# Dilated attention inside a float32 trunk: scores of two steps issued together, transposes by query tile, one shared set of four banks, and the dilation-16 groups one step ahead

## The chip, the cores and the metric

The kernel runs on one core of a Trainium2 chip. The metric is the device time of one execution in microseconds. Engines go by short names: TensorE (PE in the profile, PEld for its weight loads), VectorE (DVE), ScalarE (ACT), GpSimd (POOL) and SyncE (SP, which issues DMA transfers). An instruction that needs another engine's result waits for a semaphore. PSUM is the memory that TensorE writes; here it is divided into eight banks of 512 float32 columns.

## The reference, cut to what matters

The model is a trunk of two layers for one sequence of 1024 positions with 1024 channels, everything in float32. A layer is a token mixer and a squared-ReLU MLP, each modulated by a conditioning vector. The first mixer is a gated spatial MLP, the second is attention over three dilation patterns, which is where the change lies:

```python
B_HEADS, B_HEAD_DIM = 16, 64
B_PATTERNS = ((128, 1), (512, 4), (2048, 16))          # (window, dilation)
qkv = (h @ w_qkv).reshape(B, S, N_PAT, 3, B_HEADS, B_HEAD_DIM)
...
# dilated_branch, for one pattern: positions are split by their remainder modulo the dilation;
# a block of `span` = window // dilation queries sees its own and the previous block of keys
s = einsum('bnqrhe,bnkrhe->bnrhqk', qb, kb) * E ** -0.5
s = where(valid, s - slopes * dilation * diff, NEG)
m = max(s); p = exp(s - m); l = sum(p)
o = einsum('bnrhqk,bnkrhe->bnqrhe', p / l, vb)
lse = m + log(l)
...
wts = softmax(stack(lses))                             # over the three patterns
o = sum(wts * stack(outs)); return o.reshape(B, S, -1) @ w_out
```

## The kernel before

**Stages.** The program runs the gated MLP mixer, the first squared-ReLU MLP, attention and the second squared-ReLU MLP one after the other. Large products are made from float32 values split in a high and a low part (three matmuls for each product), and by a scheme of seven instead of eight half-size products. `attention` starts with the values of all heads (`values_stage`). Then everything else of attention is woven into one stream.

**The stream.** `project` (L1262) makes q and k for 24 groups: 8 pairs of heads, and for each the patterns of dilation 16, 4 and 1 in this order (`g` = 2, 1, 0). It is a generator. Each `next(stream)` issues three matmuls (`psqk`, L1351) and whatever ends with them: copies of a product's bank by ScalarE (`part`, L1329) or additions by VectorE (L1339), the building of a later weight operand (`left`: a cast on ScalarE, L103, and a subtraction on VectorE, L104). In this text such a step of three matmuls is a *unit*. A group has 28 units. Products that belong to one sum accumulate in one bank, so a product can wait until the copy of the bank's earlier state is done.

**The order table.** Attention itself is written into a table, `todo[step][pos]`, with 7 positions a step and 4 steps a group. `at(step, pos)` appends a function to a place. The main loop goes through the table: at each place it runs the functions there and then one unit of the stream. Group `n` has `base = 4 * n`. So the work of group `n` runs beside the projection of a later group. Once the stream is exhausted, chains of the output projection (`psd_wo`) take the place of its units. Instructions passed to `pe()` keep the order in which they are written, on their own engine; the softmax instructions (`soft`) and the copies out of banks are not held in this way.

**One step of attention.** For the near patterns (`attend`, dilation 4 and 1) a step `m` has two query tiles of 128 rows. `scores(m)` (L1616) makes scores of both heads, in two `sc` banks. For each tile and head, `soft` follows: one VectorE reduction (L1528) and one ScalarE exponential (L1530). `transposes(m, e)` (L1627, L1631) turn the probabilities of head `e` on TensorE into a `tr` bank, and a copy (L1639) brings them to SBUF; before the change the two places are one step after the scores, at positions 4 and 5, and the tile is filled by key tile, so that it also needs the next query tile's probabilities. `weighted(m)` (L1656) multiplies with the values, into the `pv` bank. For dilation 16 (`attend_far`) there are two larger steps of 64 by 64 matmuls (L1549, L1560, L1571).

**The merge.** When the three patterns of a pair are done, `merge` reads back the softmax statistics through device memory (`mst`), computes the factors (L1704 to L1716), writes them out and loads them again broadcast over rows (`bc`, two buffers), scales the three outputs (L1732; one on GpSimd, two on VectorE), adds them (L1737) and splits the sum (L103, L104). This runs beside the next pair's dilation-16 group and the first steps of its dilation-4 group; the last pair's merge runs beside the output projection. Small side jobs multiply rows of the output weight and of the residual by vectors (L1786) at fixed places.

Of the kernel before, what the change touches and what calls it, by code (L numbers as in the profile page):

```python
# [18 lines left out]
P = 128  # L19
S = 1024  # L20
D = 1024
NT = S // P
KD = D // P
HALF = 512
# [12 lines left out]
def trunk(ctx: ExitStack, tc: tile.TileContext, x, c, ada_w, ada_b, ln_g, ln_b, a_w_in, a_b_in,  # L37
# [1170 lines left out]
    def attention(before):  # L1208
# [16 lines left out]
        with ExitStack() as ph:  # L1225
# [244 lines left out]

            open_psum(ph, "B", sc=2, tr=2, mm=2, mb=1, pv=1)
            qp = pool(ph, "attn", 2)
# [59 lines left out]
            def attend_far(n, oT_of):  # L1532
# [22 lines left out]
                def transposes(h):  # L1555
                    pst = bank("tr", f"pT_{hp}_{g}_{h}")
                    for e in range(2):
                        for j in range(2):
                            o = (2 * e + j) * P
                            pe(T.transpose(pst[:, o : o + P], state["p", h][e][:, j * P : (j + 1) * P], ident[:]))  # L1560
                    t = state["pT", h] = qp.tile([P, HALF], F32, name=f"pTs_{hp}_{g}_{h}", tag="pT", bufs=6)
                    A.copy(t[:], pst[:])

                def weighted(h):
                    sums = [bank(kind, f"pv{s}_{hp}_{g}_{h}") for s, kind in enumerate(("pv", "tr"))]
                    for j in range(2):
# [14 lines left out]
                for h in range(2):  # L1581
                    at(base + 2 * h + 1, 0)(lambda h=h: scores(h))
                    at(base + 2 * h + 2, 2)(lambda h=h: transposes(h))
                    at(base + 2 * h + 3, 0)(lambda h=h: weighted(h))

                @at(base + STEPS, 1)
                def statistics():
                    for b in range(2):
                        nc.sync.dma_start(st_dram[hp, g].rearrange("s e (q b n) -> q (s e) b n", b=2, n=NT)[:, :, b, :],
                                          state["stat"][64 * b : 64 * b + 64].rearrange("p s e n -> p (s e) n"))  # L1590

            def attend(n, oT_of):
# [5 lines left out]
                probs, pT, state = {}, {}, {}  # L1598
                blocks = {m: [(t, (g == 0 and t < NT - 1) or (g == 1 and t % 2 == 0)) for t in (2 * m, 2 * m + 1)] for m in range(STEPS)}

# [3 lines left out]
                def scores(m):  # L1604
                    if m == 0:
                        state["stat"], state["bias"] = new_state(n)
                    scb = [bank("sc", f"sc_{2 * hp + e}_{g}_{m}") for e in range(2)]
                    stat, used, spans = state["stat"], 0, []
                    for t in (2 * m, 2 * m + 1):
                        w = 2 * P if has[t] else P  # L1610
                        sl = slice(used, used + w)
                        used += w
                        k0 = (t - 1) * P if has[t] else t * P
                        for e in range(2):
                            rows = slice(e * HEAD, (e + 1) * HEAD)
                            pe(T.matmul(scb[e][:, sl], my["q"][rows, t * P : (t + 1) * P], my["k"][rows, k0 : k0 + w],  # L1616
                                        start=True, stop=True))
                            spans.append((t, e, w, sl))
                    for t, e, w, sl in spans:
                        pr = probs[e, t] = qp.tile([P, 2 * P], F32, name=f"p_{2 * hp + e}_{g}_{t}", tag="p", bufs=8)  # L1620
                        col = (t % 2) * 4 + t // 2 if g == 1 else t
                        soft(pr[:, 0:w], scb[e][:, sl], state["bias"][e][:, width - w :], stat, e, col)

                def flip(pst, m, e, o):
                    for t, nxt in blocks[m]:
                        pr = probs[e, t]
                        pe(T.transpose(pst[:, o : o + P], pr[:, P : 2 * P] if has[t] else pr[:, 0:P], ident[:]))  # L1627
                        pT[e, t] = o
                        o += P
                        if nxt:  # L1630
                            pe(T.transpose(pst[:, o : o + P], probs[e, t + 1][:, 0:P], ident[:]))  # L1631
                            o += P
                    return o

                def transposes(m, e):
                    pst = bank("tr", f"pT_{2 * hp + e}_{g}_{m}")
                    end = flip(pst, m, e, 0)
                    t = qp.tile([P, HALF], F32, name=f"pTs_{2 * hp + e}_{g}_{m}", tag="pT", bufs=6)
# [3 lines left out]
                def weighted(m):  # L1642
# [3 lines left out]
                    pv = state["pv"]  # L1646
                    pieces = []
                    if m == 2 and blocks[1][1][1]:
                        pieces.append((3, 4 * P, pT[0, 3] + P, P))
                    for t, nxt in blocks[m]:  # L1650
                        pieces.append((t, t * P, pT[0, t], P * (1 + (nxt and t % 4 < 3))))
                    for n_, (t, q0, o, w) in enumerate(pieces):
                        for e in range(2):
                            rows = slice(e * HEAD, (e + 1) * HEAD)
                            o_ = o - pT[0, t] + pT[e, t]
                            pe(T.matmul(pv[rows, q0 % HALF : q0 % HALF + w], my["v"][:, t, rows], pT["tile", e, t // 2][:, o_ : o_ + w],  # L1656
                                        start=m % 2 == 0 and n_ == 0, stop=m % 2 == 1 and n_ == len(pieces) - 1, skip_group_check=True))
# [9 lines left out]

                for m in range(STEPS):
                    at(base + m, 0)(lambda m=m: scores(m))
                    at(base + m + 1, 4)(lambda m=m: transposes(m, 0))  # L1670
                    at(base + m + 1, 5)(lambda m=m: transposes(m, 1))
                    at(base + 3 + m // 2 * 2, 0)(lambda m=m: weighted(m))

                @at(base + STEPS - (n == len(order) - 1), 6 if n == len(order) - 1 else 1)
                def statistics():
                    d, stat = st_dram[hp, g], state["stat"]
                    if g == 0:
                        pst = bank("tr", f"pstat_{hp}")
                        pe(T.transpose(pst[0:32, 0:P], stat[:].rearrange("p s e n -> p (s e n)"), ident[:]))
# [7 lines left out]
            def merge(hp, oTs):  # L1687
# [120 lines left out]
            def scaled_row(i):  # L1808
# [4 lines left out]

                @at(base + 2, 5)
                def store():
# [157 lines left out]
```

## Time and profile before

| what | value |
|---|---|
| median of 3 runs | 2616.63 us (2616.61 to 2620.3) |
| profiled execution, its own time | 2611.85 us |
| its span | 2610.1 us, granted TensorE clock 0.997 |
| up to the first unit in a row of the stream | 1207.15 us |
| stream of projection and attention, 1207.15 to 1863 | 655.85 us, TensorE busy 654.94 |
| end of attention's stream and output projection, 1863 to 1953 | 90.0 us, TensorE busy 86.18 |
| after it, to the end | 657.1 us, TensorE busy 642.25 |

In the profile's rows for instructions the columns are start, duration, engine, line, operation, output and inputs, shapes, and how many equal instructions follow one another; in square brackets stands how long the engine was idle before and what ended that. `x8` scores are four matmuls in the code, since each leaves two records. A row of the waits view has the waiting engine, tile and line, what it waited for, the total in us, the count and the longest. A row of the windows view has a stretch, its length, and the busy time of each engine in it.

### The profile page before, as it was taken

The numbers are of one execution on the slowest core, as the hardware profiler recorded it, in microseconds if no ns is written. First come the engines' busy times: TensorE is split into PE (matmuls) and PEld (weight loads), VectorE is DVE, ScalarE is ACT, GpSimd is POOL, SyncE is SP. The second block draws the span as 40 slices with busy tenths as digits, with TensorE's granted clock in tenths as the row PEclk, the third lists the DMA queues.
The fourth block names the chain that finished last, engine by engine and source line by source line (L and its number), as shares of the span: only waits on it lengthen the run. The fifth ranks groups of instructions, "written<-read, shape, count | busy, mean of one in ns | idle before, by whom it ended". The sixth has DMA issues, their size and how long they took to land.

```text
span 2610.1 us, 36711 instructions
## 1 busy us (share of the span) xinstructions
PE 2561.9 (98%) x13226; PEld 2058.5 (79%) x13226; DVE 1902.3 (73%) x3506; ACT 1267.7 (49%) x2448; POOL 132.8 (5%) x201
## 2 busy tenths in 40 slices
PE   6999999999999999999999999999999999999998
PEld 5788878887788888888777777777777888878886
DVE  6767798877879678444677677776669856577987
ACT  3333385555444445333555556655417655544432
POOL 1001000000000001011010101110100000000000
PEclk9999999999999999999999999999999999999999
DMA  8553346666955744442354445454953754594562
GB/s 267 164 158 110 126 140 228 226 222 226 333 174 189 229 140 151 153 156 97 91 151 128 109 125 152 124 148 134 337 153 114 232 176 155 172 331 153 187 208 80
DMA packets 327291, 453.37 MB, mean 174 GB/s; under 512 B 51468, under 2 KB 177844, under 8 KB 327108
## 3 DMA queue, kind: packets, MB, share of 16 engines
q1 hardware_dynamic: 314244, 406.45, 48.9%
q0 software_dynamic: 12864, 44.57, 4.8%
q8 instruction: 103, 1.69, 0.3%
q14 instruction: 80, 0.66, 0.1%
HBM read 342.33 MB, written 108.61 MB: 173 GB/s over the span
## 4 chain that ended last, share of the span: by engine, by line
PE 85%; DVE 7%; DMA 4%; ACT 2%; issue 1%; SPq 0%; DVEq 0%; ACTq 0%
PE psd L1095 23%; PE psqk L1351 17%; PE psua L937 10%; PE psv L1424 9%; PE psuc L937 5%; PE psu L329 3%; DMA adaw<-in_ada_w_dram 3%; PE psd_wout L329 3%; PE psd_wo L329 3%; PE psub L937 2%; PE sc L1616 2%; PE pv L1656 2%; PE psv L522 1%; PE pT L1627 1%; DVE right L104 1%; DVE left L104 1%
## 5 line engine op out<-in xcount | busy, mean ns | idle before, releaser
L1351 PE MATMUL psqk<-right,left 128*128 128x512 f32 x2016 | 521.9, 404 | 0.9 <-ACT part L1329 0.9
L1351 PEld LDWEIGHTS psqk<-right,left 128*128 128x128 f32 x2016 | 362.0, 188 | 93.2 <-issue 15.3
L937 PE MATMUL psua<-right,left 128*128 128x512 f32 x1536 | 365.8, 391 | 3.2 <-ACT right L103 1.8
L1095 PE MATMUL psd<-rhi,lhi 128*128 128x512 f32 x896 | 349.3, 390 | 2.5 <-ACT part L968 2.5
L1095 PE MATMUL psd<-rlo,lhi 128*128 128x512 f32 x896 | 348.8, 389 | 0.1
L1095 PE MATMUL psd<-rhi,llo 128*128 128x512 f32 x896 | 348.7, 389 | 0.0
L937 PEld LDWEIGHTS psua<-right,left 128*128 128x128 f32 x1536 | 287.4, 188 | 65.4 <-ACT right L103 2.6
L104 DVE TENSOR_TENSOR left<-ws,left 128x512 fp32r<-128x512 f32 x224 | 153.8, 688 | 145.9 <-ACT left L103 144.2
L1424 PE MATMUL psv<-vwhi,right 128*128 128x512 f32 x672 | 209.8, 393 | 0.0
L1530 ACT ACTIVATE p<-p,stat 128x256 f32<-128x256 f32 (+2 forms) x384 | 161.8, 423 | 92.8 <-DVE stat L1528 91.5
L1095 PEld LDWEIGHTS psd<-rhi,lhi 128*128 128x128 f32 x896 | 168.2, 188 | 38.2 <-ACT part L968 3.3
L1095 PEld LDWEIGHTS psd<-rlo,lhi 128*128 128x128 f32 x896 | 168.2, 188 | 35.4 <-DVE rlo L104 0.7
L1095 PEld LDWEIGHTS psd<-rhi,llo 128*128 128x128 f32 x896 | 168.2, 188 | 34.8
L103 ACT CAST left<-ws 128x512 fp32r<-128x512 f32 x224 | 138.0, 620 | 110.6 <-DVE ws L858 78.3
L937 PE MATMUL psuc<-right,left 128*128 128x512 f32 x768 | 189.6, 393 | 0.5 <-ACT right L103 0.4
L937 PEld LDWEIGHTS psuc<-right,left 128*128 128x128 f32 x768 | 143.9, 189 | 30.9 <-DVE right L104 0.9
L129 DVE SCALAR_TENSOR_TENSOR adaacc<-adaw,silu_c,adaacc 128x512 f32<-128x512 f32 x140 | 107.3, 767 | 63.9 <-DMA adaw<-in_ada_w_dram 63.2
L1424 PEld LDWEIGHTS psv<-vwhi,right 128*128 128x128 f32 x672 | 126.0, 188 | 28.0 <-ACT vwhi L103 0.2
L1528 DVE CUSTOM_DVE_ANT_0 p<-sc,bias 128x256 f32<-128x256 f32 (+2 forms) x384 | 103.6, 325 | 54.2 <-PE sc L1616 54.1
L104 DVE TENSOR_TENSOR llo<-lraw,lhi 128x1024 fp32r<-128x1024 f32 x112 | 136.3, 1217 | 1.4 <-ACT lhi L103 1.4
L1424 PE MATMUL psv<-vwlo,right 128*128 128x512 f32 x336 | 131.9, 394 | 0.2 <-DVE r L216 0.2
L103 ACT CAST lhi<-lraw 128x1024 fp32r<-128x1024 f32 x112 | 117.3, 1047 | 6.2 <-PE psua L937 5.2
(271 smaller groups left out, 4333.5 us busy)
## 6 DMA issues: line engine op xcount, KB each, us to landing
lraw<-forms SPq DMA_DIRECT2D x112, 512.0 KB, 4.3
adaw<-in_ada_w_dram SPq DMA_DIRECT2D x192, 256.0 KB, 3.4
up<-in_mlp_w_up_dram SPq DMA_DIRECT2D x64, 512.0 KB, 4.2
forms<-s SPq DMA_DIRECT2D x128, 256.0 KB, 2.1
rraw<-in_mlp_w_down_dram SPq DMA_DIRECT2D x64, 512.0 KB, 4.4
forms<-part SPq DMA_DIRECT2D x96, 256.0 KB, 2.8
vraw<-in_b_w_qkv_dram SPq DMA_DIRECT2D x42, 512.0 KB, 3.8
spill<-acc SPq DMA_DIRECT2D x24, 512.0 KB, 2.6
```

Of the source, the lines that this page charges most:

```text
L103: first = A.copy(hi, src) if hi_engine is A else hi_engine.tensor_copy(hi, src)
L104: return first, lo_engine.tensor_tensor(lo, src, hi, op=ALU.subtract)
L129: ins = V.scalar_tensor_tensor(acc[:], raw[:], silu_c[:, k : k + 1], acc[:], ALU.mult, ALU.add)
L329: T.matmul(dst, s[a], m[b], start=(n == 0), stop=(n == last))
L937: T.matmul(acc, w[:, a, k, :], right[p][:, b, k, :], start=p in (1, 2, 5) and k + a + b == 0, stop=k == 3 and a == 1, skip_group_check=True)
L1095: T.matmul(sums[kind, m][:], l[a][:, k, m * P : (m + 1) * P], r[b][:, k, :], start=p in (1, 5, 2, 3) and kp + k + a + b == 0, stop=kp == K ...
L1351: ins = T.matmul(sums[kind][:], w[:, a, k, :], right[p][:, b, k, :], start=p in (1, 2, 5) and k + a + b == 0, stop=k == 3 and a == 1, skip ...
L1424: T.matmul(sums[own, m][:], right[p][:, b, 2 * kp + k, m * P : (m + 1) * P], w[a][:, k, :], start=new and k + a + b == 0, stop=kp + k == 2 ...
L1528: V.tensor_tensor_reduce(out=pr, in0=src, in1=bias, scale=-0.125, scalar=3e38, op0=ALU.add, op1=ALU.min, accum_out=nm)
L1530: A.activation(pr, pr, AF.Exp, bias=nm, scale=-1.0, accum_out=l)
L1616: pe(T.matmul(scb[e][:, sl], my["q"][rows, t * P : (t + 1) * P], my["k"][rows, k0 : k0 + w], start=True, stop=True))
L1656: pe(T.matmul(pv[rows, q0 % HALF : q0 % HALF + w], my["v"][:, t, rows], pT["tile", e, t // 2][:, o_ : o_ + w], start=m % 2 == 0 and n_ == ...
```

## The change

- **Banks.** The kinds `sc` and `tr`, two banks each, become one kind `sc` with four banks. Transposes, the second far sum and the transpose of the statistics take their banks from it too.
- **Far groups.** Scores, transposes, weighted sums and statistics of dilation 16 come one step earlier each; their distances to one another stay.
- **Near groups.** `scores(2b)` and `scores(2b+1)` are both at position 0 of one step. The softmax instructions move to a function of their own, `softs`: for the even step at position 0, for the odd one at position 2. The even step's transposes come in the same step at positions 5 and 6, the odd step's in the next step at 2 and 3. Both weighted sums are two steps after their scores, at position 0. In the first half of each dilation-4 group (`late`) the second scores stay a step later, with transposes at positions 4 and 5 of that step.
- **Transposes by query tile.** `flip` transposes each query tile's own pieces; a list `pieces` tells `weighted` which columns belong to which key tile. Dilation 1 has two more pieces than before, of the same columns in all.
- **Merge and side jobs.** Statistics go out one step earlier (for the last group five positions earlier). Of the merge, the first VectorE scaling moves from position 1 of step 2 to position 6, the others by two to three positions. The side jobs' multiplications go from positions 1 and 3 to 4 and 5, and what follows them moves with them.

```diff
-            open_psum(ph, "B", sc=2, tr=2, mm=2, mb=1, pv=1)
+            open_psum(ph, "B", sc=4, mm=2, mb=1, pv=1)
...
 # attend_far
-                    at(base + 2 * h + 1, 0)(lambda h=h: scores(h))
-                    at(base + 2 * h + 2, 2)(lambda h=h: transposes(h))
-                    at(base + 2 * h + 3, 0)(lambda h=h: weighted(h))
-                @at(base + STEPS, 1)
+                    at(base + 2 * h, 0)(lambda h=h: scores(h))
+                    at(base + 2 * h + 1, 2)(lambda h=h: transposes(h))
+                    at(base + 2 * h + 2, 0)(lambda h=h: weighted(h))
+                @at(base + STEPS - 1, 1)
                 def statistics():
...
 # attend
+                    state["spans", m] = scb, spans
+
+                def softs(m):
+                    scb, spans = state.pop(("spans", m))
                     for t, e, w, sl in spans:
                         pr = probs[e, t] = qp.tile([P, 2 * P], F32, name=f"p_{2 * hp + e}_{g}_{t}", tag="p", bufs=8)
...
+                def flip(pst, m, e):
+                    pieces = state["pieces", m] = []
+                    o = 0
+                    for t in (2 * m, 2 * m + 1):
                         pr = probs[e, t]
+                        for b in range(1 + has[t]):
+                            pe(T.transpose(pst[:, o : o + P], pr[:, b * P : (b + 1) * P], ident[:]))
+                            key = t if b == has[t] else t - 1
+                            if pieces and pieces[-1][0] == key:
+                                pieces[-1][3] += P
+                            else:
+                                pieces.append([key, t * P, o, P])
                             o += P
                     return o
...
-                for m in range(STEPS):
-                    at(base + m, 0)(lambda m=m: scores(m))
-                    at(base + m + 1, 4)(lambda m=m: transposes(m, 0))
-                    at(base + m + 1, 5)(lambda m=m: transposes(m, 1))
-                    at(base + 3 + m // 2 * 2, 0)(lambda m=m: weighted(m))
-
-                @at(base + STEPS - (n == len(order) - 1), 6 if n == len(order) - 1 else 1)
+                for b in range(2):
+                    now = base + 2 * b
+                    late = g == 1 and b == 0
+                    for m in (2 * b, 2 * b + 1):
+                        own = now + (late and m == 1)
+                        at(own, 0)(lambda m=m: scores(m))
+                        at(own, 0 if m % 2 == 0 or late else 2)(lambda m=m: softs(m))
+                        step, pos = (now + 1, 4 if late else 2) if m % 2 else (now, 5)
+                        for e in range(2):
+                            at(step, pos + e)(lambda m=m, e=e: transposes(m, e))
+                        at(now + 2, 0)(lambda m=m: weighted(m))
+
+                @at(base + STEPS - 1, 1)
                 def statistics():
...
 # merge: scale on GpSimd, scale, scale, add, add, keep
-                places = ((2, 0), (2, 1), (2, 3), (2, 5), (2, 6)) if end else ((2, 0), (2, 1), (3, 2), (3, 5), (4, 1), (4, 3))
+                places = ((2, 0), (2, 1), (2, 3), (2, 5), (2, 6)) if end else ((2, 0), (2, 6), (3, 4), (3, 5), (4, 4), (4, 6))
...
 # side jobs
-                    @at(step, 1 + 2 * n)
+                    @at(step, 4 + n)
                     def half(w=slice(n * HALF, (n + 1) * HALF)):
...
-                @at(base + 2, 5)
+                @at(base + 2, 6)
                 def high():
...
-                @at(base + 3, 1)
+                @at(base + 3, 4)
                 def low():
...
-                @at(base + 2, 5)
+                @at(base + 2, 6)
                 def store():
```

More of the change, by code (lines that the diff above doesn't have):

```diff
@@ L1555, in transposes @@
                 def transposes(h):
-                    pst = bank("tr", f"pT_{hp}_{g}_{h}")
+                    pst = bank("sc", f"pT_{hp}_{g}_{h}")
                     for e in range(2):
@@ L1564, in weighted @@
                 def weighted(h):
-                    sums = [bank(kind, f"pv{s}_{hp}_{g}_{h}") for s, kind in enumerate(("pv", "tr"))]
+                    sums = [bank(kind, f"pv{s}_{hp}_{g}_{h}") for s, kind in enumerate(("pv", "sc"))]
                     for j in range(2):
@@ L1598, in attend @@
                 probs, pT, state = {}, {}, {}
-                blocks = {m: [(t, (g == 0 and t < NT - 1) or (g == 1 and t % 2 == 0)) for t in (2 * m, 2 * m + 1)] for m in range(STEPS)}
                 if n > 0:
@@ L1607, in scores @@
                     scb = [bank("sc", f"sc_{2 * hp + e}_{g}_{m}") for e in range(2)]
-                    stat, used, spans = state["stat"], 0, []
+                    used, spans = 0, []
                     for t in (2 * m, 2 * m + 1):
@@ L1621, in scores @@
                         col = (t % 2) * 4 + t // 2 if g == 1 else t
-                        soft(pr[:, 0:w], scb[e][:, sl], state["bias"][e][:, width - w :], stat, e, col)
-                def flip(pst, m, e, o):
-                    for t, nxt in blocks[m]:
-                        pr = probs[e, t]
[L1627 to L1631, printed above, removed]
+                        soft(pr[:, 0:w], scb[e][:, sl], state["bias"][e][:, width - w :], state["stat"], e, col)
+                def flip(pst, m, e):
+                    pieces = state["pieces", m] = []
+                    o = 0
+                    for t in (2 * m, 2 * m + 1):
+                        pr = probs[e, t]
+                        for b in range(1 + has[t]):
[5 more added lines that the diff above has]
+                                pieces.append([key, t * P, o, P])
                             o += P
@@ L1635, in transposes @@
                 def transposes(m, e):
-                    pst = bank("tr", f"pT_{2 * hp + e}_{g}_{m}")
-                    end = flip(pst, m, e, 0)
+                    pst = bank("sc", f"pT_{2 * hp + e}_{g}_{m}")
+                    end = flip(pst, m, e)
                     t = qp.tile([P, HALF], F32, name=f"pTs_{2 * hp + e}_{g}_{m}", tag="pT", bufs=6)
@@ L1646, in weighted @@
                     pv = state["pv"]
[L1647 to L1651, printed above, removed]
+                    pieces = state["pieces", m]
                     for n_, (t, q0, o, w) in enumerate(pieces):
@@ L1654, in weighted @@
                             rows = slice(e * HEAD, (e + 1) * HEAD)
-                            o_ = o - pT[0, t] + pT[e, t]
-                            pe(T.matmul(pv[rows, q0 % HALF : q0 % HALF + w], my["v"][:, t, rows], pT["tile", e, t // 2][:, o_ : o_ + w],
+                            pe(T.matmul(pv[rows, q0 % HALF : q0 % HALF + w], my["v"][:, t, rows], pT["tile", e, m][:, o : o + w],
                                         start=m % 2 == 0 and n_ == 0, stop=m % 2 == 1 and n_ == len(pieces) - 1, skip_group_check=True))
```

2 lines of the change are left out of this document (1 added, 1 removed).

## The prediction, made before the result was known

> **What bounds the kernel now.** I read the page's busy shares first, then its chain of waits, then the busy time of each engine by head pair.
>
> ```profile
> span 2610.1 us, 36711 instructions
> PE 2561.9 (98%) x13226; PEld 2058.5 (79%) x13226; DVE 1902.3 (73%) x3506; ACT 1267.7 (49%) x2448; POOL 132.8 (5%) x201
> PE 85%; DVE 7%; DMA 4%; ACT 2%; issue 1%; SPq 0%; DVEq 0%; ACTq 0%
> L1351 PE MATMUL psqk<-right,left 128*128 128x512 f32 x2016 | 521.9, 404 | 0.9 <-ACT part L1329 0.9
> 1400.67:1484.27 83.60, 83.60 (x577) 63.66 (x576) 58.86 (x174) 48.04 (x145) 8.30 (x13) 1.00 0.45 128
> 1484.27:1567.85 83.58, 83.58 (x576) 63.63 (x576) 58.53 (x168) 47.84 (x144) 8.27 (x13) 1.00 0.46 128
> 1567.85:1652.16 84.31, 83.90 (x578) 63.59 (x576) 62.12 (x180) 50.07 (x148) 9.28 (x15) 1.00 0.48 139
> 1735.70:1820.12 84.42, 83.92 (x580) 63.62 (x576) 62.12 (x181) 50.22 (x148) 9.30 (x15) 1.00 0.50 140
> ```
>
> The last four rows are the windows of four head pairs: length, then the busy time of TensorE, its weight loads, VectorE, ScalarE, GpSimd, then granted clock and DMA. TensorE is busy in all 83.6 us of a pair, at clock 1.00; the projection (psqk) waited 0.9 us in the whole run. A pair gets shorter only if TensorE gets less to do or spends less per instruction; a late operand or bank makes it longer. VectorE is busy 59 of 84 us, so a TensorE wait from there comes from the order of VectorE's work, not its amount.
>
> **Scores in one burst.** The edit changes no matmul shape, only how often TensorE passes from 128-row projection matmuls to the 64-row scores and back. What such a passage costs comes from the TensorE timeline:
>
> ```profile
> 1207.15 25.70 PE L1351 MATMUL psqk<-right,left 128*128 128x512 f32 x111
> 1232.78 0.69 PE L1549 MATMUL sc<-k,q 64*64 64x64 f32 x32
> 1429.12 1.64 PE L1351 MATMUL psqk<-right,left 128*128 128x512 f32 x6
> 1430.70 0.93 PE L1616 MATMUL sc<-k,q 64*128 64x128 f32 x8
> 1431.55 3.04 PE L1351 MATMUL psqk<-right,left 128*128 128x512 f32 x12
> 1434.43 0.27 PE L1627 MATMUL pT<-ident,p 128*128 128x128 f32 x1
> 1434.54 0.27 PE L1631 MATMUL pT<-ident,p 128*128 128x128 f32 x1
> 1460.39 1.14 PE L1616 MATMUL sc<-k,q 64*128 64x256 f32 x8
> 1461.46 2.79 PE L1351 MATMUL psqk<-right,left 128*128 128x512 f32 x11
> ```
>
> Alone, psqk goes at (1232.78 − 1207.15) / 111 = 0.231 us each. From 1429.12 to 1434.43 are 5.31 us, with 18 psqk (4.16) and one score burst, which so costs 1.15. What of that is streaming? The burst of dilation 4 takes 0.85 start to start, the one of dilation 1 takes 1.07 with two more blocks of 128 columns: 0.11 a block, 0.65 for its six. The rest, 0.50, is passage, less about 0.1 that I put down to the transposes just ahead: 0.40. Lower end: all of the 0.85 is streaming, passage 0.30, less the same 0.1, 0.20. Upper end 0.50.
>
> How many go? Per head pair, position 0 holds ten bursts before (six start with weighted sums, four are scores alone) and seven after (six and one): in both near groups the second scores of a pair of steps ride behind the first, except in the first two steps of dilation 4 ("late"). Three fewer in each of 8 pairs: 24 × 0.40 = **−9.6 us** (−4.8 to −12.0).
>
> A rule bears on it. The Trainium skill, "TensorEngine Tiling (Array Packing)", Key Properties, says that a change of tiling mode, not just of tile, drains the array. By it both score steps share a mode and every merged burst saves one passage each way, so the sum would be the one above; were nothing drained, the first term would go. The 0.40 sides with the rule, but no row here shows two score steps in a row.
>
> **Transposes by query tile.** Each piece of probabilities is transposed once before and after, at the same 0.11 us (1434.43 to 1434.54). Weighted sums in dilation 1 go from 9 to 11 pieces of the same 15 column blocks; I price the extra matmuls at zero to 0.05 us each (16 records a pair at most, +0.5 us a pair if the upper end held), and take zero, because pieces follow one another within the burst without a passage.
>
> **Statistics one step earlier.** Two windows above are 0.73 and 0.84 us longer than the 83.58 of their neighbour. Why:
>
> ```profile
> 1567.39 0.18 DVE L1704 TENSOR_TENSOR mm<-mst 128x16 f32<-128x16 f32 x1 [1.01 <-DMA mst<-st_dram]
> 1572.75 0.56 ACT L1329 COPY part<-psqk 128x512 f32<-128x512 f32 x1
> 1573.37 1.66 PE L1351 MATMUL psqk<-right,left 128*128 128x512 f32 x6 [0.41 <-ACT part L1329]
> PE psqk L1351 <- ACT part L1329: 0.9, 2, 0.5
> ```
>
> The merge factors wait 1.01 us for the statistics' trip through memory; behind them on VectorE stand the far softmax reductions, behind those eight exponentials on ScalarE, and behind these the copy of the projection's bank (1572.75), for which TensorE idles. The change sends dilation 1's statistics off about a step (6 us) earlier, more than the 1.01: both events go, **−1.5 us** (0 at worst). For the last pair the statistics are ahead by about five positions too.
>
> ```profile
> 1937.51 0.50 PE L329 MATMUL psd_wo<-wo_hi,oTs 128*128 128x512 f32 x1 [1.64 <-DVE acc L1895]
> 1950.16 0.70 PE L329 MATMUL psd_wo<-wo_hi,oTs 128*128 128x512 f32 x2 [1.06 <-DMA wo_hi<-wo_dram]
> ```
>
> The first wait may shrink with the earlier last merge, the second is a weight load that nothing moves. Between 0 and −1.6; I take the middle, **−0.8**.
>
> **What becomes late.** Slack is given up. Before, transposes came eleven units (three psqk each, 0.69 us) after their scores, 7.6 us; after, five units for the first of a burst (3.5 us), and four (2.8) for the second of the late pair. Here is what softmax needs, in dilation 4's first two steps, where the last pair's merge runs on VectorE, and in an ordinary step (last two rows):
>
> ```profile
> 1410.62 1.21 DVE L1732 TENSOR_TENSOR oT<-oT,bc 128x1024 f32<-128x1024 f32 x1
> 1417.13 0.93 PE L1616 MATMUL sc<-k,q 64*128 64x128 f32 x8
> 1417.60 1.22 DVE L1732 TENSOR_TENSOR oT<-oT,bc 128x1024 f32<-128x1024 f32 x1
> 1419.33 1.22 DVE L1737 TENSOR_TENSOR oT<-oT,oT 128x1024 f32<-128x1024 f32 x1
> 1420.47 0.28 DVE L1528 CUSTOM_DVE_ANT_0 p<-sc,bias 128x128 f32<-128x128 f32 x1
> 1421.58 0.50 ACT L1530 ACTIVATE p<-p,stat 128x256 f32<-128x256 f32 x1
> 1424.09 0.93 PE L1616 MATMUL sc<-k,q 64*128 64x128 f32 x8
> 1425.12 1.22 DVE L104 TENSOR_TENSOR oT<-oT,oT 128x1024 fp32r<-128x1024 f32 x1
> 1426.86 0.59 DVE L1576 COPY oT<-pv 128x256 f32<-128x256 f32 x1
> 1427.29 0.27 DVE L1528 CUSTOM_DVE_ANT_0 p<-sc,bias 128x128 f32<-128x128 f32 x1
> 1428.39 0.49 ACT L1530 ACTIVATE p<-p,stat 128x256 f32<-128x256 f32 x1
> 1433.39 0.49 ACT L1530 ACTIVATE p<-p,stat 128x256 f32<-128x256 f32 x1
> 1433.89 0.49 ACT L1530 ACTIVATE p<-p,stat 128x256 f32<-128x256 f32 x1
> ```
>
> The first transposes need three of a step's four exponentials, those a unit later the fourth. In the ordinary step the third ends at 1433.88 and the fourth at 1434.38, 2.3 and 2.8 us after the scores (1431.63): inside 3.5. With merge work ahead the first reduction starts 2.4 us after the scores (1418.06 to 1420.47), and the third exponential ends at 1422.08, 4.0 after; in the next step 1425.02 to 1428.88, 3.9. Kept as they are, these overrun 3.5 by 0.5 and 2.8 by 1.1: 1.6 us a pair.
>
> The new places of the merge don't take this away. The second scaling waits for its broadcast, whose buffer the first one frees (1410.62 and 1417.60, 7.0 us apart): with the first at position 6 it again comes at about the end of dilation 4's first scores, and the addition with it. The last addition and the split are traced behind that step's reductions, as their runs at 1421.6 and 1425.1 were, but the split (1.22) now stands right ahead of the second step's. The far group's copy (0.59, at 1426.86) moves from the second step to the first. What eases it: TensorE's first stall is time for VectorE, so the second is shorter by up to the first, and factors no longer share a step with far reductions. I take half of 1.6, S = 0.8; the ends are 0 and 2.6 (1.6 plus 1.0, if both steps' transposes had to wait for the fourth exponential, 0.50 after the third). Seven pairs merge there: **+5.6 us** (0 to +18).
>
> The far groups' shift leaves their distances as they were; their first scores come one step nearer to their projection, whose copies have a step to spare. The four shared banks go round in turn: a transpose gets a bank whose reductions are over, and waits for their exponentials anyway. Side rows (multiplications of output weights and residual rows) only change position on VectorE; the 24 us that it has free in a pair hide them, and without that cover they add to S.
>
> Sum: −9.6 − 1.5 − 0.8 + 5.6 = −6.3. The profiled execution took 2611.85 us (span 2610.1 and 1.75 around it), 4.8 below the median shown, 2616.63; against the median the change gives **2610.3**, in the profiled execution's own terms 2605.5. A measurement of this kernel tells 0.2%, 5.2 us, from no change: faster is below 2611.4, slower above 2621.9.
>
> **Rivals.** *VectorE's backlog takes it back*: S stays 1.6 in seven pairs, +11.2; −11.9 + 11.2 = −0.7, **2615.9**, no change. For it: the merge's five VectorE operations of 1.22 us keep their number and all lie within three steps; against: each stall shortens the next.
>
> *The stalls vanish*: with S = 0, −11.9, **2604.7**. For it: VectorE has a third of its time free; against: the broadcast's 7.0 us.
>
> *Merged bursts save little*: if each step of scores pays most of its passage again, for its new banks, 24 × 0.1 is left; −2.4 − 1.5 − 0.8 + 5.6 = +0.9, **2617.5**. For it: no row shows two score steps together; against: 0.11 for every further block within a burst.
>
> *Slower: evictions behind eight exponentials.* In even steps of the near groups two softmaxes now follow one another on ScalarE. The projection's next product but one accumulates in a bank that must be copied first, four units (2.8 us) later. Row 1573.37 shows what eight exponentials of 64 columns, 0.33 us apart, do: 0.41 us of idle TensorE. With 256 columns they come 0.50 apart (1433.39, 1433.89), 1.3 us more for eight; where a quarter of that reaches TensorE too, 0.7 us a burst. Three merged bursts in 8 pairs: 24 × 0.7 = +16.8; −6.3 + 16.8 = +10.5, **2627.1**. It is slower from 24 × 0.48 on. Against: the second softmax is placed two units after the first, so that copies traced between go in between, and ScalarE is busy 48 of 84 us. The Trainium skill, "TensorE: Matmul & The Clock Gate", Architectural detail, holds VectorE's and ScalarE's queues to be strictly first in, first out. By that rule a copy never overtakes exponentials, as the copy at 1572.75 didn't, and what decides is the order in which they were written.
>
> **Numbers.** Forecast 0.37, vanished stalls 0.13, backlog 0.21, little saved 0.09, slower 0.20: faster 0.50, same 0.30, slower 0.20. Range 2603.5 to 2621.5: below it lies the upper passage price without stalls (0.05), above it most of the slower case (0.15). The likeliest one's own range is 2605 to 2613.
>
> **What would show it.** Right: pair windows of about 83.2 us (82.4 without the stall); three score bursts in a pair at 0.7 us behind a first burst, not 1.15; no TensorE wait for part or merge factors in any pair. Wrong: TensorE idle ahead of transposes in dilation 4's first two steps, released by an exponential (backlog), or ahead of psqk, released by a part copy in even steps (slower); second scores that start 0.3 us or more after the first (little saved).

## The result, and the profile after

The change makes the kernel **slower**: 2641.89 us (median of 4 runs, 2639.98 to 2646.95) against 2616.62 before, a ratio of 1.0102 with a 95% interval of 1.009 to 1.0115. Forecast were 2610.3 us and a gain of 6.3; it became a loss of 25.3, outside the stated range.

The first line of the page after, windows of three head pairs from one first far score to the next (columns as in the prediction), and TensorE's two largest waits in the stream:

```profile
span 2645.2 us, 36833 instructions
1231.55:1313.96 82.41, 82.41 (x585) 64.38 (x584) 52.72 (x157) 47.91 (x145) 5.48 (x12) 1.00 0.33 89
1313.96:1400.38 86.42, 83.40 (x586) 64.28 (x584) 58.99 (x173) 47.34 (x145) 7.81 (x13) 1.00 0.46 124
1659.96:1751.92 91.96, 85.40 (x585) 65.47 (x583) 62.38 (x176) 49.47 (x147) 9.50 (x16) 0.96 0.47 128
PE pT L1633 <- ACT p L1530: 21.9, 25, 5.7
PE psqk L1351 <- ACT part L1329: 5.1, 7, 1.8
```

The first pair has no merge of an earlier pair beside it. It takes 82.41 us where the same pair took 83.60 before (1232.78 to 1316.38): the merged bursts give 1.2 us a pair, three times 0.40, as worked out. Every later pair is longer than before, by 1.9 us (86.18 against 84.30) up to 8.4 (91.96 against 83.60), and TensorE, which had no wait in a usual pair, now waits for probabilities (p) and for copies of the projection's bank (part). The span of the profiled execution is 35.1 us longer than before, more than the medians differ: the execution traced before lies 4.8 us below its median, the one traced after 5.1 above.

Where a usual pair loses its time is seen in dilation 4's first two steps, beside the same stretch of the first pair (the first four rows):

```profile
1255.58 3.70 PE L1351 MATMUL psqk<-right,left 128*128 128x512 f32 x15
...
1259.36 0.94 PE L1351 MATMUL psqk<-right,left 128*128 128x512 f32 x3
...
1262.12 3.07 PE L1351 MATMUL psqk<-right,left 128*128 128x512 f32 x12
...
1265.27 0.94 PE L1351 MATMUL psqk<-right,left 128*128 128x512 f32 x3
...
1337.84 0.93 PE L1615 MATMUL sc<-k,q 64*128 64x128 f32 x8
1338.69 3.69 PE L1351 MATMUL psqk<-right,left 128*128 128x512 f32 x15
1342.71 0.33 PE L1633 MATMUL pT<-ident,p 128*128 128x128 f32 x1 [0.33 <-ACT p L1530]
1343.59 0.44 PE L1633 MATMUL pT<-ident,p 128*128 128x128 f32 x2 [0.55 <-ACT p L1530]
1343.79 0.94 PE L1351 MATMUL psqk<-right,left 128*128 128x512 f32 x3
...
1346.55 3.07 PE L1351 MATMUL psqk<-right,left 128*128 128x512 f32 x12
1350.61 0.33 PE L1633 MATMUL pT<-ident,p 128*128 128x128 f32 x1 [1.00 <-ACT p L1530]
1351.49 0.44 PE L1633 MATMUL pT<-ident,p 128*128 128x128 f32 x2 [0.55 <-ACT p L1530]
1351.68 0.96 PE L1351 MATMUL psqk<-right,left 128*128 128x512 f32 x3
```

From the first psqk of the stretch to the psqk behind the first transposes it takes 3.78 us in the first pair (1255.58 to 1259.36) and 5.10 here (1338.69 to 1343.79); in the second step 3.15 and 5.13. That is 1.32 and 1.98, **3.30 us a pair**, where four waits of 2.43 in all are shown. The VectorE rows of the same time, and the third exponential of each step, say why:

```profile
1337.95 1.22 DVE L1740 TENSOR_TENSOR oT<-oT,bc 128x1024 f32<-128x1024 f32 x1
1339.69 1.21 DVE L1745 TENSOR_TENSOR oT<-oT,oT 128x1024 f32<-128x1024 f32 x1
1340.82 0.59 DVE L1576 COPY oT<-pv 128x256 f32<-128x256 f32 x1
1341.85 0.28 DVE L1528 CUSTOM_DVE_ANT_0 p<-sc,bias 128x128 f32<-128x128 f32 x1
1342.95 0.49 ACT L1530 ACTIVATE p<-p,stat 128x256 f32<-128x256 f32 x1
...
1348.00 1.23 DVE L104 TENSOR_TENSOR oT<-oT,oT 128x1024 fp32r<-128x1024 f32 x1
1349.74 0.28 DVE L1528 CUSTOM_DVE_ANT_0 p<-sc,bias 128x128 f32<-128x128 f32 x1
1350.85 0.49 ACT L1530 ACTIVATE p<-p,stat 128x256 f32<-128x256 f32 x1
```

The scores are done at 1338.77; the second scaling, an addition and the far copy run ahead of the first reduction, which starts 3.1 us after them; the third exponential ends at 1343.44, 4.7 us after them. In the second step the split does the same, and the third exponential ends 4.7 us after the scores again (1346.62 to 1351.34).

The last pairs lose more, the first of them by one long hole:

```profile
1668.09 0.55 POOL L1814 DMA_DIRECT2D wo_dram<-wo_raw  x1 [7.82 <-DVE wo_raw L1220]
1678.70 3.02 POOL L1740 TENSOR_TENSOR oT<-oT,bc 128x1024 f32<-128x1024 f32 x1 [2.52 <-DMA bc<-w_dram]
1681.75 1.09 SPq L1737 DMA_DIRECT2D bc<-w_dram  x2
1689.50 1.22 DVE L1740 TENSOR_TENSOR oT<-oT,bc 128x1024 f32<-128x1024 f32 x1 [5.07 <-DMA bc<-w_dram]
1694.27 0.48 PE L1633 MATMUL pT<-ident,p 128*128 128x128 f32 x1 [5.70 <-ACT p L1530]
```

An output-weight row leaves its buffer late (1668.09). The merge's broadcasts use the same two buffers, and SyncE waits 1.7 us for that store before it issues the next one. GpSimd's scaling waits 2.52 us for the broadcast that comes into this buffer, and the last broadcast is issued right behind that scaling, at 1681.75. The scaling that needs it holds VectorE for 5.07 us, with the reductions behind it.

### The profile page after: what moved, and what is told of

Read it like the earlier page. It is cut to its first block, busy times and chain, and to the rows that moved or that the text cites. A ratio compares the mean times of both kernels' runs of the same rounds, so it can differ in the third digit from the quotient of the medians.

```text
span 2645.2 us, 36833 instructions
## 1 busy us (share of the span) xinstructions
PE 2567.3 (97%) x13290; PEld 2069.7 (78%) x13290; DVE 1907.3 (72%) x3506; ACT 1261.8 (48%) x2448; POOL 130.2 (5%) x201
## 5 line engine op out<-in xcount | busy, mean ns | idle before, releaser
L103 ACT CAST rhi<-rraw 128x1024 fp32r<-128x1024 f32 x48 | 50.5, 1053 | 138.8 <-issue 113.0
```

The source lines that it names most:

```text
L103: first = A.copy(hi, src) if hi_engine is A else hi_engine.tensor_copy(hi, src)
```

## The experiments

Ratios are to the kernel before, on the same chip in the same batch. My theory at this point: **VectorE's order** makes the transposes wait, **shared row buffers** make the long holes, and **factors ahead of the far softmax** make the waits for part. Rivals: the slack of five and four units is too short in any case; the long holes are the same backlog; the waits for part come from eight exponentials alone.

**1. Merge without its sums.**

```diff
                 def scale(g, engine):
+                    if g == 0 and not end:
+                        return
...
                 def add(g):
+                    if not end:
+                        return
```

> The changed kernel without three VectorE operations of each merge but the last: the scaling of the dilation-1 output and both additions (1.22 us each) are left out, nothing else. Theory 'VectorE's order' (the scaling and an addition stand ahead of the first reductions of the dilation-4 group on VectorE, so the transposes wait): waits of TensorE for p fall from 21.9 us to under 5 us, a pair's window from 86.3 to about 83.0 us (82.4 as in the first pair, which has no merge, plus some 0.6 of waits for part), the span by about 25 us, to about 2620. Rival 'slack too short' (five and four units are too little for a softmax in any case): the waits stay above 12 us and the pair above 85. Rival 'the clock or the bursts themselves' : nothing changes.

```profile
1402.93:1487.37 84.44, 82.97 (x585) 64.28 (x583) 56.67 (x170) 47.26 (x145) 7.86 (x13) 1.00 0.46 127
```

Waits for p fell from 21.9 to 4.7 us, the window to 84.4, not 83.0; one run, 2631.18, not the 2620 expected. The total understates it: from the first psqk to the last psd_wo this execution takes 778.9 us, against 798.1 in the changed kernel and 769.9 before, so 19.2 of 28.2 us go, and the stages outside, which the edit does not touch, took 10 us longer than before. The sums cause most of the wait; the split, still in place, leaves about 0.5 us in each second step.

**2. Merge behind the scores.** Nothing left out.

```diff
-((2, 0), (2, 6), (3, 4), (3, 5), (4, 4), (4, 6))
+((2, 0), (2, 1), (4, 1), (4, 2), (4, 3), (5, 1))
```

> The changed kernel with the merge's operations kept but written behind the scores: first VectorE scaling at step 2 position 1, second scaling and both additions at step 4 positions 1 to 3 (behind the first reductions of the dilation-4 group), the split at step 5 position 1 (behind the second ones). Theory 'VectorE's order': waits for p under 6 us (some 0.2 to 0.5 us a pair in the second step, where about 5.8 us of VectorE work lie between the two steps' reductions), windows of 83.0 to 83.5 us, total about 2620 us, same as before or up to 0.2% slower. Rival 'slack too short': waits for p stay above 12 us, total above 2632.

```profile
PE pT L1633 <- ACT p L1530: 3.4, 10, 0.5
PE psqk L1351 <- DVE k L1339: 3.8, 3, 1.8
1311.87:1395.73 83.86, 83.05 (x586) 64.58 (x584) 58.49 (x171) 47.35 (x145) 7.95 (x13) 1.00 0.46 128
1733.77:1820.30 86.53, 84.01 (x586) 64.45 (x584) 61.17 (x175) 49.24 (x147) 9.02 (x15) 1.00 0.48 136
```

2624.59 us, ratio 1.0044 (1.0028 to 1.006): more than half of the loss goes with the order alone, at unchanged slack. "Slack too short" falls. The last pairs stay long: the first scaling, now early, waits there for its own broadcast (1.9 to 2.7 us), and k waits behind it.

**3. The merge's old places alone.**

```diff
-((2, 0), (2, 6), (3, 4), (3, 5), (4, 4), (4, 6))
+((2, 0), (2, 1), (3, 2), (3, 5), (4, 1), (4, 3))
```

> The changed kernel with the merge's places alone put back to those of before (step 2 position 1, step 3 positions 2 and 5, step 4 positions 1 and 3). The first scaling comes some 7 us earlier, so the broadcast for the second one is issued earlier. Theory 'VectorE's order', in the form that the new places cause it: second scaling and first addition are over before the first scores, waits for p fall to under 8 us and the total to 2620 to 2626. Rival 'the broadcast decides, not the place': second scaling and addition again land on the scores, waits for p stay at 15 us or more, total 2633 or more.

2631.51 us, 1.0072 (1.005 to 1.0095), waits for p 8.9 us: between the two forms of the theory. (The first addition's place, step 3 position 5, is the same in both kernels; the other four differ.) The new places cost about 0.3%; but with the old ones the second scaling and an addition still run ahead of the first reduction (in the third pair from 1420.83, the scores starting at 1421.21).

**4. The side jobs' old places alone.**

```diff
-                    @at(step, 4 + n)
+                    @at(step, 1 + 2 * n)
...
-                @at(base + 3, 4)
+                @at(base + 3, 1)
                 def low():
```

> The changed kernel with the side jobs' places alone put back (multiplications at positions 1 and 3, high part at 5, low part at step 3 position 1). In the changed kernel the low part of an output weight runs three positions later, and the buffer it shares with the merge's broadcasts is free later; in the pairs that start at 1660 and 1752 us the second scaling then waits 5.07 and 1.49 us for its broadcast. Theory 'shared row buffers': those waits go, the two windows fall from 92.0 and 89.6 us to about 86.5, the granted clock there goes from 0.96 and 0.98 to 1.00, the total falls by 7 to 11 us, to about 2632. Rival 'the long stall is the VectorE order alone': nothing changes by more than 3 us.

```profile
1655.79:1742.01 86.22, 83.59 (x586) 64.36 (x584) 62.15 (x175) 49.28 (x147) 9.45 (x15) 1.00 0.46 136
```

2631.99 us, 1.007 (1.0053 to 1.0087). The two long windows, 91.96 and 89.57 us, come back to 86.22 and 86.37, as in the other pairs, with the clock at 1.00; the four short waits in each pair stay (28, 17.6 us). So a second cause, worth about 0.3%; but experiment 5 shows that the late rows alone do not make the holes.

**5. Factors pinned.** Each of their instructions in `pe()`.

```diff
-                    V.tensor_tensor(m[:], nm[:, 0], nm[:, 1], op=ALU.min)
+                    pe(V.tensor_tensor(m[:], nm[:, 0], nm[:, 1], op=ALU.min))
...
```

> The changed kernel with the merge factors (L1712 to L1724) held in the order in which they are written, so that they come behind the far group's first reductions on VectorE instead of ahead of them. Theory 'factors ahead of the far softmax': in the changed kernel the factors wait for the statistics and hold the far reductions and, through them, the copy of the projection's bank; pinned, the waits for part fall from 5.1 us to under 1 us. The price: the broadcasts leave some 5 us later, the second scaling with them, so waits for p rise above 22 us and the total does not fall (2640 us or more). Rival 'the copies wait for the eight far exponentials alone': the waits for part stay at 4 us or more.

```profile
PE sc L1615 <- ACT k L1335: 4.0, 5, 1.4
1655.99:1743.29 87.30, 84.26 (x585) 65.51 (x583) 62.88 (x175) 49.75 (x147) 9.44 (x16) 0.98 0.48 135
```

One run, 2630.47. No wait for part is left, so the theory holds. Waits for p did not rise (19.0 us), nor did the total reach 2640, as I had expected; new waits for k appear. The side rows are in their new places here, and still the two long windows are 87.30 and 87.93 us, near the 86.5 to 87.1 of the others. In this run the last broadcast is issued behind VectorE's first scaling and not behind GpSimd's (the same holds for these two pairs in experiment 4). So the holes need both, late rows and early factors; why the order of the two scalings turns is not shown.

**6. Two repairs together** (2 and 4).

> The kernel with the merge behind the scores, and the side jobs' places of before as well. If the two causes (VectorE's order, shared row buffers) are separate and add up, TensorE's waits for k (3.8 us in three pairs without the second edit) go, the last windows fall from 86.1 and 86.5 to about 84 us, and the total is 6 us under that of the one with the first edit alone: about 0.2% above before (ratio 1.001 to 1.003). If the long windows of the last pairs had another cause, the ratio stays at 1.004.

2608.66 us, ratio **0.9986** (0.9975 to 0.9997), better than expected: faster than the kernel before. Alone the repairs give 0.6 and 0.3 points, together 1.2: in the last pairs the early first scaling, which waited 1.9 to 2.7 us for its broadcast in experiment 2, waits 0.5 at most here.

**7. All three repairs.** Also with the second addition behind the second step's reductions, and with the first scaling left at its new place.

```diff
-((2, 0), (2, 6), (3, 4), (3, 5), (4, 4), (4, 6))
+((2, 0), (2, 6), (4, 1), (4, 2), (5, 1), (5, 2))
```

> All three repairs: merge behind the scores (first scaling at step 2 position 6, second scaling and first addition at step 4 positions 1 and 2, second addition and split at step 5 positions 1 and 2), side jobs as before, factors pinned behind the far reductions. If the three causes are all that stands against the merged bursts, waits for part and p together are under 3 us in the stream, windows are 82.5 to 83.2 us against 83.6 before, and the total is 4 to 8 us under before: ratio 0.997 to 0.9985. If later broadcasts now hold VectorE in another place, windows stay above 83.6 and the ratio at 1.000 or more.

```profile
PE sc L1615 <- ACT k L1335: 5.6, 7, 1.1
1329.78 2.40 DVE L1292 TENSOR_TENSOR ws<-wk,wk 128x512 f32<-128x512 f32 x1
1332.99 0.62 ACT L103 CAST left<-ws 128x512 fp32r<-128x512 f32 x1 [3.20 <-DVE ws L1220]
```

2618.18 us, 1.0017 (1.0008 to 1.0026). The last clause of the expectation came true: waits for p are 1.4 us and for part 0.7, but every pair now waits for k. The rows show a new reason. GpSimd's scaling, late with the factors, runs from 1329.22 to 1331.62. A sum for a weight operand (ws) that starts on VectorE meanwhile takes 2.40 us, where it takes 0.68 elsewhere. The next sum is late by as much, ScalarE's cast waits 3.20 us for it, and the copy of k stands behind the cast.

**8. Two repairs, and the second addition behind the reductions**, factors free again.

```diff
-((2, 0), (2, 6), (3, 4), (3, 5), (4, 4), (4, 6))
+((2, 0), (2, 1), (4, 1), (4, 2), (5, 1), (5, 2))
```

> As the kernel with the merge behind the scores and the side jobs' places of before, but the second addition also behind the second step's reductions (step 5 position 1, split at position 2). By the theory of VectorE's order the remaining waits for p (3.0 us in seven pairs, each with about 0.5 us of lost time beside it) go: waits for p under 1 us, windows of pairs 82.5 to 83.3 us, total 3 to 6 us under that kernel, ratio to before 0.996 to 0.998. If the later split holds ScalarE or the output's buffers, windows stay at 83.3 and the ratio at 0.9986 or above.

```profile
1391.49:1474.20 82.71, 82.59 (x586) 64.60 (x584) 58.66 (x174) 47.30 (x145) 8.04 (x13) 1.00 0.45 129
```

2610.89 us, **0.9984** (0.9974 to 0.9994). The first pair takes 82.45 us, the next four 82.60 to 83.12, where a pair without a wait took 83.6 before: 0.5 to 1.0 of the 1.2 us stays there. The total is not clearly better than in experiment 6; the last pairs (83.47 and 84.05) still wait for part (2.0 us in three).

**9. One burst split.** In the kernel of experiment 8:

```diff
-                    late = g == 1 and b == 0
+                    late = True
```

The expectation misreads this edit: the shift also asks for `m == 1`, so only the first half of dilation 1 was split, one burst a pair and not three.

> The same kernel with every half of a near group treated as the late one: the second scores of each pair of steps stay a step later, so there are ten score bursts in a pair again, as before the change; all else is equal. This prices the merged bursts alone. Theory (0.40 us of passage for each burst that goes, 24 of them): every window is 1.2 us longer, total 9 to 10 us above the kernel with merged bursts, so 2 to 5 us above before. Rival 'merged bursts gain nothing in the full program because evictions come late behind eight exponentials': the difference is under 4 us.

2620.73 us, 1.0021 (1.0011 to 1.003). The first window is 82.80 us, 0.35 for one burst. The total says more than that one burst, since the last softmaxes moved as well; it prices nothing by itself.

**10. All bursts single.** As 9, and

```diff
-                        own = now + (late and m == 1)
+                        own = now + m % 2
```

> The kernel with both additions behind the reductions, now with the second scores of every pair of steps really a step later: the shift goes by m % 2. (In the run named single bursts the shift stayed with m == 1, so it split only the first half of dilation 1 and left two of the three merged bursts of a pair; its first window, 82.80 against 82.45 us, is the price of one.) Ten bursts of scores a pair, as before the change. Theory (0.40 us of passage each): the first window is 1.2 us longer, 83.6 us as before the change, the total 9 to 10 us above the kernel with merged bursts, plus whatever waits the other placing of the softmaxes brings. Rival 'a good part of the 1.2 us comes from the transposes by query tile or the shared banks': the first window stays under 83.2 us.

2636.82 us, 1.0085 (1.0071 to 1.0098). The edit brought a wait of its own: the statistics' transpose now came too soon behind the last softmax, 1.79 us in every pair. Inconclusive.

**11. The same, statistics of the near groups a step later, as before the change.**

```diff
-                @at(base + STEPS - 1, 1)
+                @at(base + STEPS - (n == len(order) - 1), 6 if n == len(order) - 1 else 1)
                 def statistics():
```

> The kernel with all scores in bursts of their own, and the statistics of the near groups a step later, where they were before the change. In the run without this the transpose of the statistics stood on TensorE eight units behind the last scores and waited 1.79 us in every pair, which hid the price of the bursts. Theory (0.40 us of passage a burst): no wait for the statistics, first window 83.6 us as before the change, against 82.45 with merged bursts; total some 10 us above the kernel with merged bursts, ratio to before 1.000 to 1.003. Rival 'part of the 1.2 us is not the bursts': first window under 83.2 us. As a second reading: with the statistics later, the merge factors should again come behind the far reductions, and the waits for part fall under 1 us.

```profile
1229.65:1313.26 83.61, 83.61 (x584) 63.86 (x583) 52.42 (x155) 48.48 (x145) 5.48 (x12) 1.00 0.32 87
PE sc L1615 <- ACT k L1335: 14.4, 7, 3.8
1331.99 1.22 DVE L1740 TENSOR_TENSOR oT<-oT,bc 128x1024 f32<-128x1024 f32 x1 [1.03 <-DMA bc<-w_dram]
1334.12 2.90 POOL L1740 TENSOR_TENSOR oT<-oT,bc 128x1024 f32<-128x1024 f32 x1 [5.28 <-DMA bc<-w_dram]
1334.82 2.76 DVE L1220 TENSOR_TENSOR ws<-ws,wq 128x512 f32<-128x512 f32 x1
1337.66 0.62 ACT L103 CAST left<-ws 128x512 fp32r<-128x512 f32 x1 [4.66 <-DVE ws L1220]
```

The first window is 83.61 us, just that of before: the whole 1.2 us is the bursts, and the rival that transposes or banks have a part in it falls. There is no wait for part any more (2.5 us in three pairs in experiment 10), and the factors now run behind the far reductions: the earlier statistics bring them ahead. The total, 2640.01 us or 1.0098 (1.0082 to 1.0114), missed the expected 1.000 to 1.003: the later factors send the broadcasts later, the scaling at step 2 waits (1.03 us here, up to 2.91), and behind it a ws sum meets GpSimd's scaling and takes 2.76 us, as in experiment 7; the cast and the copy of k follow late.

**12. Dilation 4's first half merged as well.** In the kernel of experiment 8:

```diff
-                    late = g == 1 and b == 0
+                    late = False
...
-((2, 0), (2, 1), (4, 1), (4, 2), (5, 1), (5, 2))
+((2, 0), (2, 1), (4, 3), (4, 4), (5, 1), (5, 2))
```

> The same kernel with the first half of dilation 4 merged too (no late half; second scaling and first addition of the merge at step 4 positions 3 and 4, behind both softmaxes): six bursts a pair. Theory: one more passage of 0.40 us a pair goes, first window 82.0 us, 8 x 0.40 = 3.2 us off the kernel with seven bursts, ratio to before about 0.997, if VectorE's two softmaxes in a row still end ahead of the transposes. Rival 'the slack there is too short for two softmaxes and the merge': waits for p of 0.5 us or more in each of seven pairs, ratio 0.999 or above.

```profile
PE sc L1615 <- DVE oT L1576: 7.1, 7, 1.6
1253.34 2.13 PE L1615 MATMUL sc<-k,q 64*128 64x128 f32 x16
```

2621.38 us, 1.0025 (1.0014 to 1.0036). Neither gain nor the rival's wait, but a third thing: the second scores need a bank that the far group's second sum has just filled, and wait for its copy. In the first pair, 82.60 us and so no shorter than with seven bursts, the new burst takes 2.13 us where the next, at 1268.09, takes 1.58. With four shared banks, this is what the `late` half avoids.

## Why the prediction was wrong

- **Scores in one burst: right.** −9.6 forecast; 82.41 against 83.60 in the first pair, and experiment 11 gives it back. A merged burst takes 1.51 us up to the next psqk (1269.32 to 1270.83), a single one 0.86: the second scores add 0.65, the streaming that the prediction priced, and no passage, so "little saved" falls. That these pairs hold the same transposes and weighted sums also bears out the zero for transposes by query tile: experiment 11 keeps them and takes 83.61.
- **What becomes late: wrong in size, and with it in sign.** The step that failed is "I take half of 1.6, S = 0.8". The bound of 2.6 was too low as well: S was 3.30 in a usual pair, +23 us in seven instead of +5.6. The overrun itself was mis-sized: the third exponentials end 4.7 us after their scores in both steps, not 4.0 and 3.9, so that slacks of 3.5 and 2.8 are overrun by 1.2 and 1.9, not by 0.5 and 1.1. In the first step the far copy, which the prediction saw moving there and did not price, and a weight sum behind it push the reductions from 2.4 us behind the scores to 3.1. The reason for halving didn't hold either: the first stall did not shorten the second (1.32, then 1.98): VectorE itself then stood idle for 1.42 us, up to 1345.05, waiting for a cast on ScalarE, before it went on to the second addition and the split. That VectorE's queue order, not its load, decides was said in the prediction's first part; the price left it out. The late place of the second scaling was foreseen, but its broadcast's buffer is freed by GpSimd's scaling here (1417.26 to 1419.67; broadcast at 1419.70), not by VectorE's first one: that it came out at the same place was luck.
- **Statistics one step earlier: wrong in sign.** The factors' wait for statistics was not removed: it was there in two of seven pairs and is in six now (0.21 to 1.70 us). Factors run ahead of the far reductions in all seven pairs, as before; but the copy of the bank behind them is now due sooner after the far scores, which came a step earlier. Before, TensorE waited only where the reductions started more than 2.2 us after the far scores began; now it waits in every pair, by what their start exceeds 1.4 us (here 2.51, and 1.12 of wait):

```profile
1400.23 0.18 DVE L1712 TENSOR_TENSOR mm<-mst 128x16 f32<-128x16 f32 x1 [1.00 <-DMA mst<-st_dram]
1402.89 0.23 DVE L1528 CUSTOM_DVE_ANT_0 p<-sc,bias 128x64 f32<-128x64 f32 x1
1405.87 0.56 ACT L1329 COPY part<-psqk 128x512 f32<-128x512 f32 x1
1406.49 2.36 PE L1351 MATMUL psqk<-right,left 128*128 128x512 f32 x9 [1.12 <-ACT part L1329]
```

  It is the chain of the prediction's rows at 1567.39, now in all seven pairs: waits for part 5.1 us instead of 0.9. "their first scores come one step nearer to their projection, whose copies have a step to spare" overlooked this copy. "Factors no longer share a step with far reductions" took the table's place for the instruction's; factors are not held in the written order, and ran about a step ahead of theirs.
- **Side rows: wrong.** Free VectorE time did not cover their move, because what they hold is a buffer. The prediction looked at neither that buffer nor the store on GpSimd's queue (1668.09) that frees it. Experiment 4 prices it at 0.3%, with experiment 2's repair at about 0.6% (1.0044 to 0.9986); by experiment 5 it takes early factors too.
- **Shared banks: right for this change**, by the `late` half alone, as experiment 12 shows.
- **Last merge:** −0.8 was expected from the wait of 1.64 us behind an addition; it is 1.81 after. Not there.
- **The rivals.** The backlog on VectorE was the right mechanism at less than half its price. The slower rival, evictions behind eight exponentials of the near groups, wasn't found: all seven waits for part lie in far steps. The slower side came from the backlog, which I had capped at S = 1.6.

In the traced executions the stream, from the first psqk to the first psd_wo, lasts 687.64 us against 656.04, 31.6 more. With S = 3.3, +5 for part and some 9 for the two long holes, −9.6 + 23 + 5 + 9 = +27; the last pair's merge, beside the stream's end, costs 3.8 more than a usual one (7.8 against 4.0, over the pace of the first pair), which makes +31. The output projection behind the stream is 3.4 shorter, so attention grew by 28.2, and the rest of the 35.1 lies in stages that the change does not touch. The 25.3 between the medians is not split up by any trace.

## What to carry to other kernels

When work is moved closer to its producer, the slack must be checked against the worst step, behind everything that may stand ahead in the other engine's queue, and a stall is to be priced at the late end until something shown shortens it. A table of places is not the order of instructions: what isn't held in order may come a step earlier, ahead of what it was to follow. A side job that seems free on its engine can still hold a buffer that the main chain needs, and an operation moved on one engine can slow another engine's work that it now meets.

## What the runs showed of the hardware beyond expectation

**The clock.** The long hole cost more than its length. TensorE was idle from about 1688.6 to 1694.27; the rows are windows of 1 us (the last of 2 us) of the changed kernel, columns as above, with the granted clock third from the end:

```profile
1692.00:1693.00 1.00, 0.00 (x0) 0.00 (x0) 1.00 (x3) 0.00 (x0) 0.00 (x0) 0.57 0.99 288
1697.00:1698.00 1.00, 1.00 (x6) 0.90 (x5) 1.00 (x2) 0.62 (x1) 0.00 (x0) 0.50 0.56 163
1699.00:1700.00 1.00, 1.00 (x10) 0.67 (x10) 0.95 (x3) 0.51 (x1) 0.00 (x0) 1.00 0.00 0
1784.00:1786.00 2.00, 1.45 (x5) 1.15 (x5) 0.75 (x3) 2.00 (x8) 0.00 (x0) 0.58 0.49 194
```

The clock went to 0.50 some 3.5 us into the idle time and came back at 1699, so the first 4.7 us of work ran at half rate: up to 2.3 us lost on top of the 5.7. The Trainium skill, "TensorE: Matmul & The Clock Gate", What's actually happening, says that the array's clock halves after an idle window of about 3.4 us and returns after as much sustained work; in this hole the trace agrees with the first and shows 4.7 us for the second. But shorter waits lowered the clock too: it is 0.58 in the last row, behind a wait of 0.95 us and, 6 us later, one of 2.10, and 0.50 from 1850 to 1852, behind a single wait of 1.79.

**VectorE beside GpSimd.** In the streams of the 14 traces, some 70 additions, subtractions and scalings of VectorE that read both operands from SBUF started while GpSimd ran a scaling of the merge. All of them ended 0.54 to 0.62 us after GpSimd's, but for one of 1024 columns, 1.08 after: the rest of GpSimd's time was added to them, up to 2.2 us. Some 40 others, which read one operand from a PSUM bank (L1339), started beside it as well and kept their time of 1.06 to 1.10 us. In the kernel before, what lies beside GpSimd's scaling reads mostly banks; in experiments 7 and 11 it meets the ws sums.
